# Token-order probabilities, merged operand splits and a 25th block chunk in a hybrid convolution and attention layer

## The chip, the cores and the metric

The kernel runs on one NeuronCore of a Trainium2 chip. The metric is the device time of one execution in microseconds (us). The engines are named as the profile names them: PE multiplies matrices, PEld loads its stationary operand, DVE is the vector engine, ACT the scalar engine, POOL and SP here mostly issue transfers. SBUF is the on-chip memory of 128 partitions, PSUM the eight banks of 128 x 512 float32 into which PE writes.

## The reference

One layer on 512 latent tokens of width 1024 (an 8 x 64 grid) and 256 context tokens. RMS norm and modulation give `h` and `hc`; one input projection gives ten parts; a gated short convolution is branch A, neighbourhood attention branch B; both are projected, merged by sigmoid gates, projected again and added to `x`.

```python
parts = _split_in(h @ w_in)            # b, c, x, z_a, q, k, v, z_b, g_a, g_b: 1024 columns each
q, k = rope(q), rope(k)                # 16 heads of 64
k_c, v_c = split(hc @ w_in[:, K_OFF:V_END])
# query (row r, col c) sees all 8 rows x 16 columns clip(c-8, 0, 48)..+15, and all 256 context keys
p = softmax([q.k_nb * scale + rel_bias, q.k_c * scale])
attn = p_nb @ v_nb + p_c @ v_c
y_a = (silu(z_a) * b * conv3(c * x)) @ w_out_conv
y_b = (silu(z_b) * attn) @ w_out_attn
out = x + gt * rmsnorm((sigmoid(g_a) * y_a + sigmoid(g_b) * y_b) @ w_o)
```

## The kernel before, in words

**Precision.** Every float32 operand is split into a high part H (a rounded copy, type float32r, made on ACT, line 68) and a low part L = x - H (a subtraction on DVE, line 71). A product is then three matmuls, H.H, H.L and L.H. `split` (lines 64 to 76) is that pair of operations, so each split is one ACT and one DVE operation, the second waiting for the first.

**Chunks.** The weights come in chunks of 1024 x 256 (two units of 128 output columns), 40 of them from `win` and 8 from `wout`, in the order that the list `order` writes out. Each chunk is four DMAs on SP's queue into `ring`, which holds one and a half chunks. A plain chunk is split by two 128x1024 operations (`Chunk.split`) and multiplied by `unit`/`proj_T` (lines 174 to 176): per unit 8 x 3 matmuls of 128x512. A block chunk is cut into 2 x 2 blocks (B11, B12, B21, B22), and `pair` forms both units from seven products instead of eight, in the manner of Strassen and Winograd: seven `product` calls of 12 matmuls of 128x256 (line 299). Its operands are B11, B21, the sums T1 and T2 (`Chunk.first`, made ahead of time) and T3, T4, B22 (`Chunk.second`, made when the pair begins); the sums are DVE additions in place in `ring` (lines 112 to 120; line 129 for the chunks below). A pair has a first half (B11, B21, T1, T2, on three banks `a`, `b`, `e`) and a second (T4, T3, B22); ACT copies banks out (lines 310 to 321), DVE adds (lines 316 to 327). Five chunks, of the query and key pairs 1, 2, 3, 4 and 6, also need the plain B12 (`keep`): there B12 must be split before B22 is added to it in place. 24 chunks go in blocks; `paired` decides which.

**Operand buffers.** Split operands lie in four buffers `w` of 128 x 2048: a block chunk takes two in `first` and two in `second`, so those of the next chunk come free as the pair's halves end.

**Attention.** For each pair of heads p (0 to 7) and head h, four blocks b of 128 queries. A query block sees 32 grid columns, which are two key tiles of 128 keys, and two tiles of context keys. The blocks are shifted by 64 queries against the token order, block 3 holding the last 64 and the first 64. `scores` (line 723, 732) multiplies, DVE adds the bias and takes the maximum (line 739), ACT takes the exponential (746, 750) and scales (753). `turn2` transposes the 128x128 pieces on PE (line 760) and splits them into TH and TL, indexed by query block and tile. `gather` multiplies by the values: 12 matmuls (line 779), four of 128x512 for the context and eight of 128x256, each of those over two query blocks that needn't be adjacent; then it adds the two halves of the result on ACT and DVE (784, 785, and 786 for the block that wraps round). `values` splits V in pieces of 128x128, one per head pair and token tile.

**Order.** `plan` lists which projections fill PE between the attention steps of each head pair: the main loop runs one score block, one part of the fill, transposes and gathers in turn. After the loop comes `gate2(3)`, the last gate zb 3, around the last `gather`, then the merge with the gates g 2, g 3, the first output chunk y 0 and so on. Python order is only the starting point: the framework arranges each engine's instructions when the program is built, by its own estimates, and the engines then run these fixed orders, each waiting on semaphores.

Of the kernel before, what the change touches and what calls it, by code (L numbers as in the profile page):

```python
# [27 lines left out]
def layer(ctx: ExitStack, tc, xp, ctxt, ctxT, cc, wmod, small, wfirst, win, wout, wo, rel, tab, out):  # L28
# [59 lines left out]
    class Chunk:  # L88


        def __init__(self, src):
            self.raws = []
            for i in range(2):
                at = 2 * (turn[0] % 3)
                turn[0] += 1
                for o in range(2):
                    nc.sync.dma_start(ring[:, at + o], src[:, 2 * i + o])
                self.raws.append(ring[:, at:at + 2].rearrange("p u (k c) -> p u k c", k=4))
# [8 lines left out]

        def first(self, keep=False):
            (b11, b12), (b21, b22) = self.b = [(r[:, 0], r[:, 1]) for r in self.raws]
            t, sums = (wtile([P, 2, 2, 4, P]) for _ in range(2))  # L110
            split(t[:, 0, 0], t[:, 0, 1], b11)
            nc.vector.tensor_add(b11, b11, b12)
            split(sums[:, 0, 0], sums[:, 0, 1], b11)
            split(t[:, 1, 0], t[:, 1, 1], b21)
            nc.vector.tensor_add(b11, b11, b22)
            split(sums[:, 1, 0], sums[:, 1, 1], b11)
            self.keep = keep
            if not keep:
# [124 lines left out]
    def paired(n, i):  # L243
        return n == "g" or n == "v" and i == 1 or n == "qk" and i in (1, 2, 3, 4, 6) or n == "zb" and i < 3 or n in ("cx", "bz") and i > 3
# [141 lines left out]
    with ExitStack() as p0:  # L386
# [80 lines left out]
        with tc.manual_schedule(engines={E.PE, E.DVE, E.Activation, E.SP}):  # L467
# [58 lines left out]
            kept(1, wide[1])  # L526
# [121 lines left out]
    def values(g):  # L648
        w = chunk()
        for p in (2 * g, 2 * g + 1):  # L650
            V[p] = aw.tile([P, 6, 2, P], F32R, name="V", bufs=3)
        for t in range(6):
            ps = pj()
            n = t % 4
            proj_N(ps, w, hx if t < 4 else hc, slice(n * P, (n + 1) * P))
            vs = summed(ps)
            for i, p in enumerate((2 * g, 2 * g + 1)):
                src = vs[:, i * P:(i + 1) * P].rearrange("p (h d) -> p h d", h=2)
                split(V[p][:, t, :, 0:64], V[p][:, t, :, 64:P], src)
            if t % 2:  # L660
                yield
# [49 lines left out]

    def scores(p, h, b):
# [42 lines left out]

    def turn2(pts, b, TH, TL):
        tps = [psT().rearrange("p (c q) -> p c q", c=4) for _ in pts]
        for tp, pt in zip(tps, pts):
            for c in range(4):
                nc.tensor.transpose(tp[:, c], pt[:, c * P:(c + 1) * P], ident)  # L760
        for n, tp in enumerate(tps):
            split(TH[:, b + n], TL[:, b + n], tp)

    def gather(p, h, TH, TL):
# [12 lines left out]
        for n, (kt, dst, src) in enumerate(work):  # L777
            for t in (TH, TL):
                nc.tensor.matmul(  # L779
                    o3[:, dst], lhsT=V[p][:, kt, h], rhs=src(t),  # L780
                    start=n == 0 and t is TH, stop=n == len(work) - 1 and t is TL,
# [3 lines left out]
        nc.vector.tensor_add(attn[p][r, 64:512], o[r, :448], tmp[r, :448])  # L785
        nc.vector.tensor_add(attn[p][r, 0:64], o[r, 448:], tmp[r, 448:])
# [68 lines left out]
    for i, (p, h, b) in enumerate(blocks):  # L855
# [388 lines left out]
```

## Time and profile before

| | before |
|---|---|
| median of 3 runs | 703.33 us (702.55 to 703.91) |
| the profiled execution, its time and its span | 702.33 us and 700.5 us |
| DVE in 492 to 528 us (zb 3, g 2, g 3) | 31.78 us busy of 36 |
| DVE in 450 to 475 us | 24.75 us busy of 25 |
| granted PE clock, mean | 0.998 |

The profile is of one execution; its span runs from the first to the last instruction, and 1.8 us lie around it. PE's records overlap: a matmul of 128x256 has a record of 283 ns, but in a stream the next one starts about 120 ns later. So start-to-start times are used for PE, and for DVE and ACT either the mean duration of one operation, or the start-to-start time where they follow each other without a wait.

### The profile page before, as it was taken

Reading aid. Unit: us, or ns where it says so; the run is one execution under the profiler, and the core shown is the slowest. Engines: PE = TensorE matmul, PEld = TensorE weight load, DVE = VectorE, ACT = ScalarE, POOL = GpSimd, SP = SyncE. Lnnn points to the kernel's source line nnn. Section 1 sums busy time; section 2 is a strip of 40 time slices with the busy share of each in tenths; the row PEclk is TensorE's granted clock in tenths of the full one; section 3 lists DMA queues with packets and bytes.
Section 4 is the critical chain, followed back from the end, with each engine's and each line's share of the span. In section 5 each row is a group of like instructions: output and inputs, shape, how many; then the busy total and the mean of one; then the engine's idle time right before and its main releaser. Section 6 shows DMA issues by size and latency. Waiting matters only on the chain.

```text
span 700.5 us, 12059 instructions
## 1 busy us (share of the span) xinstructions
PE 690.8 (99%) x4340; PEld 622.7 (89%) x4340; DVE 609.5 (87%) x1184; ACT 448.3 (64%) x905; POOL 66.6 (10%) x110
## 2 busy tenths in 40 slices
PE   7999999999999999999999999999999999999996
PEld 5888888899989999898999989999898899988885
DVE  6999998799898999877999697999799787775996
ACT  7568542677688687675877757787694444442563
POOL 0000003122040310402103113000000000000000
PEclk9999999999999999999999999999999999999999
DMA  9995955347263463543635436334464445660013
GB/s 354 406 350 192 314 168 128 77 114 186 81 152 108 111 181 125 113 144 82 165 119 136 111 104 160 95 112 143 149 222 136 146 146 175 232 235 30 31 61 120
DMA packets 51727, 108.84 MB, mean 155 GB/s; under 512 B 6610, under 2 KB 6866, under 8 KB 51668
## 3 DMA queue, kind: packets, MB, share of 16 engines
q1 hardware_dynamic: 43202, 92.73, 39.1%
q0 software_dynamic: 8320, 15.21, 10.9%
q8 instruction: 34, 0.56, 0.3%
q14 instruction: 25, 0.20, 0.1%
q10 hardware_dynamic: 146, 0.14, 0.1%
HBM read 87.60 MB, written 5.25 MB: 133 GB/s over the span
## 4 chain that ended last, share of the span: by engine, by line
PE 97%; DMA 1%; DVE 1%; SPq 1%; ACT 0%; issue 0%; DVEq 0%; ACTq 0%
PE ps L299 34%; PE ps L174 9%; PE ps L176 9%; PE ps L175 9%; PE ps L187 6%; PE ps L1042 5%; PE ps L779 4%; PE ps L760 4%; PE ps L192 3%; PE ps L723 3%; PE ps L206 2%; PE ps L457 2%; PE ps L463 2%; PE ps L460 2%; DMA wm<-in_wmod 1%; PE ps L732 1%
## 5 line engine op out<-in xcount | busy, mean ns | idle before, releaser
L71 DVE TENSOR_TENSOR w<-ring,w 128x512 fp32r<-128x512 f32 (+1 forms) x215 | 166.0, 789 | 29.8 <-ACT w L68 28.8
L68 ACT CAST w<-ring 128x512 fp32r<-128x512 f32 (+1 forms) x215 | 144.5, 706 | 67.0 <-PE ps L176 21.6
L299 PE MATMUL ps<-S,w 128*128 128x256 f32 x1152 | 146.2, 283 | 0.0
L299 PEld LDWEIGHTS ps<-S,w 128*128 128x128 f32 x1152 | 141.7, 192 | 0.1
L299 PE MATMUL ps<-h,w 128*128 128x256 f32 x864 | 112.5, 284 | 0.0
L299 PEld LDWEIGHTS ps<-h,w 128*128 128x128 f32 x864 | 108.0, 191 | 2.0
L174 PE MATMUL ps<-h,w 128*128 128x512 f32 x144 | 56.4, 391 | 0.0
L175 PE MATMUL ps<-h,w 128*128 128x512 f32 x144 | 56.3, 391 | 0.0
L176 PE MATMUL ps<-h,w 128*128 128x512 f32 x144 | 55.9, 389 | 0.0
L631 POOL DMA_DIRECT2D tc<-tb x32 | 28.6, 1048 | 285.6 <-DVE tc L629 181.7
L753 ACT ACTIVATE pt<-pt,z 128x512 f32<-128x512 f32 x64 | 43.0, 723 | 7.5 <-DVE z L751 7.3
L68 ACT CAST TH<-ps 128x512 fp32r<-128x512 f32 x64 | 35.7, 586 | 13.8 <-PE ps L760 13.7
L71 DVE TENSOR_TENSOR TL<-ps,TH 128x512 fp32r<-128x512 f32 x64 | 42.5, 681 | 0.8 <-ACT TH L68 0.3
L739 DVE CUSTOM_DVE_ANT_1 ps<-ps,bt 128x512 f32<-128x512 f32 x56 | 38.7, 692 | 4.4 <-PE ps L723 4.3
L760 PE MATMUL ps<-ident,pt 128*128 128x128 f32 x256 | 33.3, 273 | 0.0
L187 PE MATMUL ps<-w,h 128*128 128x512 f32 x128 | 32.4, 394 | 0.0
L176 PEld LDWEIGHTS ps<-h,w 128*128 128x128 f32 x144 | 27.0, 188 | 5.7
L175 PEld LDWEIGHTS ps<-h,w 128*128 128x128 f32 x144 | 27.1, 188 | 5.5
L174 PEld LDWEIGHTS ps<-h,w 128*128 128x128 f32 x144 | 27.0, 188 | 5.5
L760 PEld LDWEIGHTS ps<-ident,pt 128*128 128x128 f32 x256 | 29.2, 140 | 2.2 <-ACT pt L753 0.4
L746 ACT ACTIVATE pt<-ps,m 128x512 f32<-128x512 f32 x32 | 22.1, 690 | 13.6 <-DVE m L739 12.9
L779 PE MATMUL ps<-TH,V 128*128 128x256 f32 (+1 forms) x96 | 28.4, 318 | 0.0
(251 smaller groups left out, 1400.5 us busy)
## 6 DMA issues: line engine op xcount, KB each, us to landing
ring<-in_win SPq DMA_DIRECT2D x148, 256.0 KB, 3.2
wm<-in_wmod SPq DMA_DIRECT2D x26, 512.0 KB, 7.4
ring<-in_wout SPq DMA_DIRECT2D x32, 256.0 KB, 3.3
bt<-in_rel SPq DMA_DIRECT2D x16, 256.0 KB, 2.7
tc<-tb POOLq DMA_DIRECT2D x32, 128.0 KB, 3.3
wg<-in_wmod SPq DMA_DIRECT2D x16, 256.0 KB, 3.1
B<-in_wo SPq DMA_DIRECT2D x8, 512.0 KB, 5.9
fraw<-in_wfirst SPq DMA_DIRECT2D x8, 384.0 KB, 8.3
```

The lines of the kernel that those rows point to most:

```text
L68: cast = nc.scalar.copy(H, src)
L71: nc.vector.tensor_sub(L, src, H.bitcast(F32))
L174: nc.tensor.matmul(ps, lhsT=H[k][:, cs], rhs=mH[k], start=k == 0, stop=False)
L175: nc.tensor.matmul(ps, lhsT=H[k][:, cs], rhs=mL[k], start=False, stop=False)
L176: nc.tensor.matmul(ps, lhsT=L[k][:, cs], rhs=mH[k], start=False, stop=k == KT - 1)
L187: nc.tensor.matmul(ps, lhsT=mH[k][:, ts], rhs=both[k].rearrange("p a c -> p (a c)"), start=k == 0, stop=False, skip_group_check=True,)
L299: nc.tensor.matmul(ps, lhsT=w[:, x, k], rhs=act[y][k], start=start and k + o == 0, stop=k == 3 and o == 2, skip_group_check=True,)
L739: nc.vector.tensor_tensor_reduce(out=s3, in0=s3, in1=bt[:, e::4 - e][:, 0:2], scale=-1.0, scalar=3.0e38, op0=ALU.add, op1=ALU.min, accum_o ...
L753: nc.scalar.mul(x, x, z[:, i:i + 1])
L760: nc.tensor.transpose(tp[:, c], pt[:, c * P:(c + 1) * P], ident)
L779: nc.tensor.matmul(o3[:, dst], lhsT=V[p][:, kt, h], rhs=src(t), start=n == 0 and t is TH, stop=n == len(work) - 1 and t is TL,)
L1042: nc.tensor.matmul(out, lhsT=a(x, k, ts), rhs=w[y][k // 2][:, k % 2, cols], start=start and k + o == 0, stop=k == 3 and o == 2, skip_group ...
```

## The change

Four edits, made together:

1. `Chunk.two` splits two operands of a chunk by one operation of 128x1024 instead of two of 128x512: B11 with B21, T3 with T4, and in the five `keep` chunks B12 with B22. It reads both from `ring` with a step, so both have to be there, and what overwrites either has to wait for the whole operation.
2. V: two token tiles are summed side by side and then split by one operation of 128x256 per head pair.
3. `turn2` stores the probabilities in token order (block 3 is transposed against a rotated identity, which POOL makes at the start), `places` lays the key tiles so that every `gather` operand is contiguous, and each inner product covers just the queries that see the tile: 192, 256, 256 and 192 instead of 256 each. The sum at the end is one operation instead of two.
4. `paired` also names zb 3: the last gate chunk goes through `pair` instead of `unit`.

```diff
         def first(self, keep=False):
...
-            split(t[:, 0, 0], t[:, 0, 1], b11)
+            self.B = {"T1": sums[:, 0], "T2": sums[:, 1]}
+            self.two(("B11", "B21"), t, (0, 0))
             nc.vector.tensor_add(b11, b11, b12)
             split(sums[:, 0, 0], sums[:, 0, 1], b11)
-            split(t[:, 1, 0], t[:, 1, 1], b21)
...
+        def two(self, names, x, us):
+            at = [a + u for a, u in zip(self.at, us)]
+            lo = min(at)
+            src = ring[:, lo:max(at) + 1:max(at) - lo].rearrange("p n (k c) -> p n k c", k=4)
+            split(x[:, :, 0], x[:, :, 1], src)
+            for n, a in zip(names, at):
+                self.B[n] = x[:, int(a > lo)]
...
         def second(self):
...
             if self.keep:
-                split(last[:, 1, 0], last[:, 1, 1], b12)
+                self.two(("B12", "B22"), last, (1, 1))
                 nc.vector.tensor_add(b12, b12, b22)
-            for n, x, b in (("T3", t[:, 0], b12), ("T4", t[:, 1], b21), ("B22", last[:, 0], b22)):
-                split(x[:, 0], x[:, 1], b)
-                self.B[n] = x
-            self.B["B12"] = last[:, 1]
+            self.two(("T3", "T4"), t, (1, 0))
+            if not self.keep:
+                split(last[:, 0, 0], last[:, 0, 1], b22)
+                self.B["B22"] = last[:, 0]
...
-        return n == "g" or ... or n == "zb" and i < 3 or n in ("cx", "bz") and i > 3
+        return n == "g" or ... or n == "zb" or n in ("cx", "bz") and i > 3
...
-        work.append((0, slice(0, 4, 3), lambda t: t[:, 0:4:3, 0]))
-        for k in range(1, 3):
-            work.append((k, slice(k - 1, k + 1), lambda t, k=k: t.rearrange("p b c q -> p (b c) q")[:, 4 * k - 3:4 * k + 1:3]))
-        work.append((3, slice(2, 4), lambda t: t[:, 2:4, 1]))
+        for kt, a, b in ((0, 0, 192), (1, 64, 320), (2, 192, 448), (3, 320, S)):
+            work.append((kt, a, b, lambda t, kt=kt, a=a, b=b: t[:, 3 * (kt % 2), a:b]))
...
-        nc.vector.tensor_add(attn[p][r, 64:512], o[r, :448], tmp[r, :448])
-        nc.vector.tensor_add(attn[p][r, 0:64], o[r, 448:], tmp[r, 448:])
+        nc.vector.tensor_add(attn[p][r], o[r], tmp[r])
```

Since the framework arranges the instructions anew, the edits move others too. Three places. In all rows the changed kernel's lines are higher by 2 to 21: 299 becomes 311, 71 becomes 73, 779 becomes 800, 723 becomes 742.

**PE, the gather of head pair 7, head 0.** Before (`TH`, `TL`: the probabilities; `h_82` to `h_85`: tokens for the first product of the next pair, g 1; `S_1242`: the last of the pair ahead, g 0):

```order
L299 MATMUL ps<-S_1242,w 128x256 x3
L779 MATMUL ps<-TH,V 128x512
L723 MATMUL ps<-ks,qd 128x512
L723 MATMUL ps<-ks,qe 128x512
L299 MATMUL ps<-h_82,w 128x256 x3
L299 MATMUL ps<-h_83,w 128x256 x3
L299 MATMUL ps<-h_84,w 128x256 x3
L299 MATMUL ps<-h_85,w 128x256 x2
L779 MATMUL ps<-TL,V 128x512
```

The same place in the changed kernel:

```order
L311 MATMUL ps<-S_1236,w 128x256 x3
L800 MATMUL ps<-TH,V 128x512
L800 MATMUL ps<-TL,V 128x512
L800 MATMUL ps<-TH,V 128x512
L800 MATMUL ps<-TL,V 128x512
L800 MATMUL ps<-TH,V 128x192
L800 MATMUL ps<-TL,V 128x192
```

Two scores and eleven matmuls that stood between the gather's first matmul and its second now stand behind the gather.

**DVE, the split operands for the second half of the chunk of query and key pair 2.** Before (`w_1960` holds B22 and B12, `w_1959` T3 and T4; line 129 is the addition in place to B12, 316 an addition of the running pair):

```order
L71 TENSOR_TENSOR TL_1767<-ps_1946,TH_1766 128x512
L71 TENSOR_TENSOR w_1960<-ring_105,w_1960 128x512
L71 TENSOR_TENSOR w_1959<-ring_105,w_1959 128x512
L129 TENSOR_TENSOR ring_105<-ring_105 128x512
L71 TENSOR_TENSOR w_1960<-ring_105,w_1960 128x512
L316 TENSOR_TENSOR tc_1970<-tc_1970,ps_1973 128x256
L71 TENSOR_TENSOR w_1959<-ring_105,w_1959 128x512
```

Now (`w_1929` holds B12 and B22, `w_1928` T3 and T4):

```order
L73 TENSOR_TENSOR TL_1740<-ps_1915,TH_1739 128x4x2x64
L73 TENSOR_TENSOR w_1929<-ring_106,w_1929 128x2x512
L328 TENSOR_TENSOR tc_1935<-tc_1935,ps_1938 128x256
L140 TENSOR_TENSOR ring_106<-ring_106 128x512
L73 TENSOR_TENSOR w_1928<-ring_106,w_1928 128x2x512
```

T4, which the second half multiplies first, was the second split and stood ahead of the addition; now it is in the last one, behind the addition.

**PE, the second half of g 3, two chunks behind zb 3, and the start of y 0** (`us`: operand of y 0). Before, three whole products, then y 0:

```order
L299 MATMUL ps<-h_86,w 128x256 x3
L299 MATMUL ps<-h_87,w 128x256 x3
L299 MATMUL ps<-h_88,w 128x256 x3
L299 MATMUL ps<-h_89,w 128x256 x3
L299 MATMUL ps<-S_943,w 128x256 x3
```

Now:

```order
L311 MATMUL ps<-h_87,w 128x256 x2
L311 MATMUL ps<-S_947,w 128x256 x2
L311 MATMUL ps<-S_944,w 128x256 x2
L185 MATMUL ps<-us_6073,w 128x512
L311 MATMUL ps<-h_87,w 128x256
L311 MATMUL ps<-h_88,w 128x256 x3
L311 MATMUL ps<-h_89,w 128x256 x3
```

The two matmuls with H of each product stand ahead, with the first of y 0, and the third, which needs L, comes after them. The same break stands in the second halves of query and key pairs 1 and 2. In the kernel before, no product of a pair is broken like this; one (g 1) is parted by a gather.

On SP's queue the loads of g 2 move behind the first half of zb 3, since a pair asks for the next chunk in its middle and a plain chunk at its start. POOL's queue gains one copy at the start and exchanges some neighbours among its transfers.

More of the change, by code (lines that the diff above doesn't have):

```diff
@@ L48, in layer @@
     sp = const.tile([P, 72], F32, name="sp")
-    ident = const.tile([P, P], F32, name="ident")
+    wide = const.tile([P, 192], F32, name="ident")
+    ident, rolled = wide[:, :P], wide[:, 64:]
     make_identity(nc, ident)
+    nc.gpsimd.tensor_copy(wide[:, P:], wide[:, :64])
     eps = const.tile([P, 1], F32, name="eps")
@@ L95, in __init__ @@
                 turn[0] += 1
+                self.at.append(at)
                 for o in range(2):
@@ L213, in proj_c, with summed @@
             )
-    def summed(ps):
-        t = cv.tile([P, S], F32, name="ta")[:, :256]
+    def summed(ps, t=None):
+        if t is None:
+            t = cv.tile([P, S], F32, name="ta")[:, :256]
         nc.scalar.copy(t, ps[:, 256:])
@@ L516, in keep_busy @@
                     nc.tensor.matmul(acc[5][:, :256], lhsT=ident, rhs=cb[:, 0, :256], start=True, stop=True)
-            wide = [spread(i) for i in range(2)]
+            spreads = [spread(i) for i in range(2)]
             square(0)
             square(1)
-            kept(0, wide[0])
+            kept(0, spreads[0])
             root(0)
@@ L525, in layer @@
             norm(1)
-            kept(1, wide[1])
+            kept(1, spreads[1])
             square(2)
@@ L655, in values @@
             proj_N(ps, w, hx if t < 4 else hc, slice(n * P, (n + 1) * P))
[L656 to L659, printed above, removed]
+            if t % 2 == 0:
+                vs = cv.tile([P, 2, 256], F32, name="ta")
+            summed(ps, vs[:, t % 2])
             if t % 2:
+                for i, p in enumerate((2 * g, 2 * g + 1)):
+                    src = vs[:, :, i * P:(i + 1) * P].rearrange("p t (h d) -> p t h d", h=2)
+                    split(V[p][:, t - 1:t + 1, :, 0:64], V[p][:, t - 1:t + 1, :, 64:P], src)
                 yield
@@ L710, in layer @@
     whole = []
+    places = [(0, 3, 1, 2), (3, 0, 1, 2), (0, 3, 1, 2), (0, 3, 1, 2)]
     def scores(p, h, b):
@@ L757, in turn2 @@
         tps = [psT().rearrange("p (c q) -> p c q", c=4) for _ in pts]
-        for tp, pt in zip(tps, pts):
+        for n, (tp, pt) in enumerate(zip(tps, pts)):
             for c in range(4):
-                nc.tensor.transpose(tp[:, c], pt[:, c * P:(c + 1) * P], ident)
+                nc.tensor.transpose(tp[:, places[b + n][c]], pt[:, c * P:(c + 1) * P], rolled if b + n == 3 else ident)
         for n, tp in enumerate(tps):
-            split(TH[:, b + n], TL[:, b + n], tp)
+            if b + n < 3:
+                ts = slice(64 + (b + n) * P, 64 + (b + n + 1) * P)
+                split(TH[:, :, ts], TL[:, :, ts], tp)
+            else:
+                H, L = (t.rearrange("p c (a q) -> p c a q", q=64)[:, :, 0::7] for t in (TH, TL))
+                split(H, L, tp.rearrange("p c (a q) -> p c a q", q=64))
     def gather(p, h, TH, TL):
@@ L769, in gather @@
         o = psO()
-        o3 = o.rearrange("p (b q) -> p b q", b=4)
-        work = [(4, slice(0, 4), lambda t: t[:, :, 2]), (5, slice(0, 4), lambda t: t[:, :, 3])]
-        work.append((0, slice(0, 4, 3), lambda t: t[:, 0:4:3, 0]))
-        for k in range(1, 3):
-            work.append((k, slice(k - 1, k + 1), lambda t, k=k: t.rearrange("p b c q -> p (b c) q")[:, 4 * k - 3:4 * k + 1:3]))
-        work.append((3, slice(2, 4), lambda t: t[:, 2:4, 1]))
-        for n, (kt, dst, src) in enumerate(work):
+        work = [(4, 0, S, lambda t: t[:, 1]), (5, 0, S, lambda t: t[:, 2])]
+        for kt, a, b in ((0, 0, 192), (1, 64, 320), (2, 192, 448), (3, 320, S)):
+            work.append((kt, a, b, lambda t, kt=kt, a=a, b=b: t[:, 3 * (kt % 2), a:b]))
+        for n, (kt, a, b, src) in enumerate(work):
             for t in (TH, TL):
                 nc.tensor.matmul(
-                    o3[:, dst], lhsT=V[p][:, kt, h], rhs=src(t),
-                    start=n == 0 and t is TH, stop=n == len(work) - 1 and t is TL,
+                    o[:, a:b], lhsT=V[p][:, kt, h], rhs=src(t),
+                    start=n == 0 and t is TH, stop=n == len(work) - 1 and t is TL, skip_group_check=True,
                 )
```

9 lines of the change are left out of this document (4 added, 5 removed).

## The prediction

> **What bounds the kernel now.** I read the page's busy times first, then the slices, the chain and PE's waits.
>
> ```profile
> PE 690.8 (99%) x4340; PEld 622.7 (89%) x4340; DVE 609.5 (87%) x1184; ACT 448.3 (64%) x905; POOL 66.6 (10%) x110
> PE   7999999999999999999999999999999999999996
> DVE  6999998799898999877999697999799787775996
> PE 97%; DMA 1%; DVE 1%; SPq 1%; ACT 0%; issue 0%; DVEq 0%; ACTq 0%
> ```
>
> ```profile
> PE ps L507 <- ACT crow L479: 3.7, 1, 3.7
> PE ps L457 <- ACT h L555: 0.3, 1, 0.3
> ```
>
> PE is full from the second slice to the last but one, the chain is PE for 97%, and after the start PE waits for nobody: those two rows are all its waits. So today every nanosecond of matmul counts and no nanosecond of DVE or ACT does. But DVE is at 87%, and at nine tenths or more in 19 of the 40 slices: PE's freedom from waits hangs on DVE finishing in the right order. The change takes from PE, and alters DVE's order and load. Both have to be priced.
>
> What a matmul costs is the distance between starts. From the timeline of PE, in y 3 and the gate chunk g 7 behind it, in a gather, and at transposes:
>
> ```profile
> 599.79 0.39 PE L174 MATMUL ps<-as,w 128*128 128x512 f32 x1
> 601.60 0.39 PE L176 MATMUL ps<-as,w 128*128 128x512 f32 x1
> 601.83 3.04 PE L299 MATMUL ps<-h,w 128*128 128x256 f32 x24
> 604.70 3.04 PE L299 MATMUL ps<-S,w 128*128 128x256 f32 x24
> ```
>
> ```profile
> 184.84 0.40 PE L779 MATMUL ps<-TH,V 128*128 128x512 f32 x1
> 185.77 0.28 PE L779 MATMUL ps<-TH,V 128*128 128x256 f32 x1
> 186.72 0.39 PE L723 MATMUL ps<-ks,qd 128*128 128x512 f32 x1
> ```
>
> ```profile
> 475.04 1.03 PE L760 MATMUL ps<-ident,pt 128*128 128x128 f32 x8
> 475.83 1.68 PE L299 MATMUL ps<-h,w 128*128 128x256 f32 x12
> ```
>
> Between the first two rows lie eight steps: 1.81/8 = 0.226 us for 512 columns. 24 matmuls of 256 take 2.87, so 0.1196 each. In the gather four of 512 take 0.93 (0.2325 each, 0.006 more than elsewhere) and eight of 256 take 0.95 (0.119). Eight transposes of 128 columns take 0.79, 0.099 each.
>
> **PE's share of the change.**
>
> *zb 3 in blocks.* 2 x 24 matmuls of 512 go: 48 x 0.226 = 10.86 us. Seven products of 12 come: 84 x 0.1196 = 10.05. Net -0.81.
>
> *192 columns.* 16 gathers have four of their matmuls narrowed from 256 to 192, 64 in all. No row shows this width in this number format. A straight line through 512 and 256 (0.00042 per column) gives 0.093: -1.7 us in all. If loading the stationary operand sets the pace it stays at 0.119: no gain. The nearest row speaks against the line: transposes have 128 columns, for which the line gives 0.066, but take 0.099. I take the middle between that row and 0.119, which is 0.109: 64 x 0.010 = -0.64. The bad end is the plain float32 rate, which the fillers at the start show:
>
> ```profile
> 11.74 1.03 PE L516 MATMUL ps<-cb,ident 128*128 128x256 f32 x4
> 12.61 0.38 PE L539 MATMUL ps<-ident,x 128*128 128x128 f32 x2
> ```
>
> Four records are two matmuls of 256 columns: 0.87/2 = 0.435 each, or 0.326 for 192; 64 x 0.207 = +13.2 us. That is a rival. The Trainium skill (TensorE: Matmul & The Clock Gate, section Back-to-back issue gap) gives a gap of columns/2.4 + 2.5 ns, 82.5 ns for 192; by that the edit would be worth 64 x 36.5 ns = 2.3 us. The trace disagrees for narrow matmuls: by the rule a transpose would be at 56 ns, its row is at 99.
>
> *Contiguous operands.* 64 matmuls of 512 in the gathers lose at most the 0.006 us: 0 to -0.4, I take -0.2, since the scores, too, read in pieces.
>
> PE alone: -0.81 - 0.64 - 0.2 = -1.65 us. The transposes keep their number and width. POOL's extra copy follows the making of the identity, which PE uses six microseconds later, and costs nothing:
>
> ```profile
> 1.02 0.29 POOL masks.py:199 TENSOR_SCALAR_AFFINE_SELECT ident<-ident 128x128 f32<-128x128 f32 x1
> ...
> 7.40 1.22 PE L516 MATMUL ps<-cb,ident 128*128 128x256 f32 x2
> ```
>
> **DVE's and ACT's share.** Durations by shape, and two runs of splits without waits:
>
> ```profile
> L71 DVE TENSOR_TENSOR w<-ring,w 128x512 fp32r<-128x512 f32 x173 | 114.9, 683 | 10.2 <-ACT w L68 9.5
> L71 DVE TENSOR_TENSOR w<-ring,w 128x1024 fp32r<-128x1024 f32 x42 | 51.1, 1222 | 19.5 <-ACT w L68 19.3
> L68 ACT CAST w<-ring 128x1024 fp32r<-128x1024 f32 x42 | 44.0, 1053 | 24.6 <-PE ps L176 12.4 <-DMA ring<-in_wout 5.4 <-DMA ring<-in_win 4.3
> L71 DVE TENSOR_TENSOR V<-ta,V 128x128 fp32r<-128x128 f32 x48 | 11.9, 285 | 3.3 <-ACT V L68 3.3
> L324 DVE SCALAR_TENSOR_TENSOR tc<-tc 128x256 f32<-128x256 f32 x16 | 6.7, 420 | 3.0 <-ACT tc L321 3.0
> L785 DVE TENSOR_TENSOR at<-ps,ta 64x448 f32<-64x448 f32 x16 | 9.9, 620 | 0.8 <-ACT ta L784 0.6
> ```
>
> ```profile
> 472.39 1.88 DVE L71 TENSOR_TENSOR w<-ring,w 128x512 fp32r<-128x512 f32 x3
> ```
>
> In a stream a DVE operation of 512 holds the engine (1.88 - 0.683)/2 = 0.60 us, its record being 0.08 longer; 1024 hold it 1.222 - 0.08 = 1.14. So a merged split saves 0.06 us of DVE, not half: 24 chunks with two merges and five with a third are 53 x 0.06 = 3.2 us. V saves (0.285 - 0.08) x 48 less 24 x 0.34, the holding time of 256 by the 420 row: 1.7. The gather's second addition goes, about 0.1 each, 1.6 in 16. On PE's path all of this is worth nothing by itself, because PE doesn't wait. What costs is that a merged operand is ready only when both are:
>
> *Query and key pair 2* (second place of the order). Its rows before:
>
> ```profile
> 182.47 0.67 DVE L71 TENSOR_TENSOR TL<-ps,TH 128x512 fp32r<-128x512 f32 x1
> 183.05 1.28 DVE L71 TENSOR_TENSOR w<-ring,w 128x512 fp32r<-128x512 f32 x2
> 187.19 1.58 PE L299 MATMUL ps<-h,w 128*128 128x256 f32 x12
> ```
>
> T4's L was ready at 184.33, 2.9 us before PE wanted it at 187.19. Now there follow on TL: the B12/B22 split 1.14, a running addition 0.34, the addition in place 0.60, then ACT's cast of 1.05 (it may not start before the addition ends) and DVE's split of 1.22. From 183.05 that is 4.35 us plus 0.1 for two handovers: 187.5. One more addition (line 112, now 125) has slipped into the stretch ahead: 188.1; DVE had no gap there before, and each new wait for an ACT cast adds, one or two of up to 1.05: 188.1 to 190. PE has nine matmuls to put ahead, 1.1 us, so it loses 0 to 1.8. I take 1.3, near the upper end, since the wait is in series with a full engine; it also covers the running pair's bank, which comes free later. The other four keep chunks have the same series with more cover: 0 to 0.9 each, I take 0.8 for all. Together 2.1 (0 to 5.4).
>
> *Gather of pair 7, head 0* (first place). Before:
>
> ```profile
> 480.22 0.40 PE L779 MATMUL ps<-TH,V 128*128 128x512 f32 x1
> 481.26 0.67 DVE L71 TENSOR_TENSOR TL<-ps,TH 128x512 fp32r<-128x512 f32 x1
> 482.23 0.40 PE L779 MATMUL ps<-TL,V 128*128 128x512 f32 x1
> ```
>
> TL was ready at 481.93, 1.7 us after the first matmul; two scores and eleven products filled that. Now TL is wanted one matmul after TH, at 480.45. If DVE is as late as before, PE stands 1.5 us; if the shorter queue ahead of TL brings it forward, 0. I take 0.8.
>
> *zb 3, g 2, g 3* (third place). DVE's load from 492 to 528 us, and its waits there:
>
> ```profile
> 492.00:528.00 36.00, 31.78 (x55) 1.00 0.55 190
> ```
>
> ```profile
> DVE us L71 <- ACT us L68: 2.1, 2, 1.7
> DVE g L324 <- ACT g L321: 1.1, 1, 1.1
> ```
>
> zb 3 before: two splits of 1024, 2.28 us. Now: two of 1024 and three of 512 (4.08), four additions in `ring` (2.4), four operations of 256 on the results (1.36): 7.84, so +5.6. Merges in g 2 and g 3 and the gather's addition take back 0.35. 31.78 + 5.2 = 37.0 us of work, while PE's work there shrinks to 35.2. DVE falls behind by 1.8 even without a gap, by 3.4 if half of the 3.2 us of waits above stays; splits for y 0 in the stretch can slip instead. 0 to 3.4, I take 1.9. The loads of g 2, now asked for in the middle of zb 3, add nothing to that:
>
> ```profile
> ring<-in_win SPq DMA_DIRECT2D x148, 256.0 KB, 3.2
> ```
>
> They land 3.2 us after their issue, and the second half of zb 3 (36 x 0.12) and the gather last 6; without that cover g 2's first split would be late by what is lacking.
>
> The Trainium skill (Perfetto Trace Analysis, section Optimizing Scalar/DVE Operations) says both things: grouping into larger operations helps a saturated engine, at about 60 ns of overhead per DVE operation on SBUF; where the engine isn't saturated but makes others wait, breaking up is better. The 0.06 us here agrees with the figure; which half applies is what the places above decide.
>
> **The sum.** Waits 2.1 + 0.8 + 1.9 = 4.8, PE -1.65: +3.15 us. On the profiled execution, 702.33 (700.5 of span and 1.8 around it), that is 705.5. The median of the runs lies 1.0 above it, so 703.33 + 3.15 = 706.5 us.
>
> **The rivals.** About 0.2%, 1.4 us, is what a measurement of this kernel can tell from no change.
>
> *The waits don't come* (faster). DVE loses 6.5 us of work outside zb 3, so it may run ahead and hide the series. For it: no wait of PE in 670 us before, and slices at 7 and 8. Against it: the order puts H matmuls ahead of late L ones in three pairs, where before it did so in none. 703.33 - 1.65 = 701.7, below 701.9. This is the grouping half of that page's rule. It decides if T4 of pair 2 is ready by about 188.4 and DVE catches up by g 3. Chance 0.13.
>
> *Half of it* (the same): waits of 0.3 to 3.0 us, 702 to 704.7. Chance 0.13.
>
> *192 columns at the float32 rate* (much slower): +13.2 instead of -0.64; DVE then has 13 us more room, so most waits go: 703.33 - 1.0 + 13.2 + 1 = 716.5. No row shows a split operand's matmul under 256 columns, so nothing excludes it; that 512 and 256 lie on one line speaks against a jump. Chance 0.07.
>
> *The forecast*, waits of over 3 us: 0.67.
>
> The range: at the low end waits of 0.8 us, 702.5. At the high end, 710.5, they come to 8.8, most of the 10.3 that the upper ends give (5.4 + 1.5 + 3.4). Left out are the best of the fast case and the 192-column rival.
>
> **What would show it.** PE records 4376. In the waits, PE rows that wait for DVE, about 5 us in sum: at the second half of pair 2, at L800 near 480, at L311 and L185 near 525 to 530. DVE busy in the stretch of zb 3 to g 3 near 100%. L800's 192 wide matmuls 0.10 to 0.12 us apart. Wrong would be: no PE waits, a 192 step of 0.09 or of 0.33, or waits at places that I did not name.

## The result and the profile after

| | before | after |
|---|---|---|
| median of the runs | 703.81 us (702.55 to 703.91, 5 runs) | 707.65 us (707.45 to 708.84, 5 runs) |
| the profiled execution, time and span | 702.33 and 700.5 us | 707.47 and 705.7 us |
| ratio | | 1.0062, 95% interval 1.0048 to 1.0076 |

Slower by 0.6%, or 4.4 us (3.4 to 5.4), against a forecast of 3.15. The two profiled executions lie 5.1 apart. The page of the changed kernel: busy times, the slices of PE and DVE, and the chain.

```profile
PE 692.7 (98%) x4376; PEld 623.6 (88%) x4376; DVE 610.9 (87%) x1102; ACT 443.5 (63%) x835; POOL 67.0 (10%) x111
PE   7999999999999999999999999999999999999996
DVE  6999998799797998977998787999999787775996
PE 69%; DVE 20%; ACT 5%; DMA 3%; issue 2%; SPq 0%; DVEq 0%; ACTq 0%
```

PE has its 4376 records and its slices look as before; DVE has 82 operations fewer and is busy 1.4 us longer. The chain tells the difference: it was PE for 97%, and now runs through DVE for a fifth of the span. PE's waits behind the 3.7 us at the start that both kernels have (the kernel before had only one other, of 0.3):

```profile
PE ps L800 <- DVE TL L73: 1.1, 2, 0.8
PE ps L311 <- ACT w L70: 0.8, 2, 0.5
PE ps L469 <- ACT h L567: 0.6, 1, 0.6
PE ps L185 <- ACT w L70: 0.5, 1, 0.5
PE ps L311 <- DVE w L73: 0.3, 1, 0.3
PE ps L779 <- ACT pt L772: 0.2, 1, 0.2
```

(L469 is that one, near the start, now 0.6.) Only 1.4 of these 3.5 us wait for DVE, the rest for ACT. This view shows less than PE loses, because a matmul's record goes on for 0.16 us after the next could start. What follows therefore uses **standing time**: over all matmul records behind the first 100 us, what the distance between two starts exceeds the median for that line and shape, where it exceeds it by over 0.13 us. Before: 0. After: 4.8 us, at twelve places, in us:

| second half of pair 2 (187.3), and transposes behind it (197.6) | 0.70, 0.35 |
|---|---|
| first half of zb 0 (241), second half of pair 4 (274) | 0.25, 0.15 |
| gather at 295 | 0.47 |
| gather of pair 7, head 0 (482.9) | 0.92 |
| g 2, g 3 and the first product of y 0 (516 to 529) | 0.17, 0.41, 0.47, 0.14, 0.61 |
| g 4 (548) | 0.18 |

Each stop costs about another 0.1 us, 1.2 in sum, since the matmul that ends it is followed late (below). The three places of the prediction, in PE's, DVE's and ACT's timelines.

Pair 2:

```profile
184.91 1.22 DVE L73 TENSOR_TENSOR w<-ring,w 128x1024 fp32r<-128x1024 f32 x1
186.04 0.41 DVE L328 TENSOR_TENSOR tc<-tc,ps 128x256 f32<-128x256 f32 x1
186.37 0.69 DVE L140 TENSOR_TENSOR ring<-ring 128x512 f32<-128x512 f32 x1
187.09 1.05 ACT L70 CAST w<-ring 128x1024 fp32r<-128x1024 f32 x1 [1.06 <-DVE ring L140]
188.17 1.23 DVE L73 TENSOR_TENSOR w<-ring,w 128x1024 fp32r<-128x1024 f32 x1 [1.11 <-ACT w L70]
188.19 0.50 PE L311 MATMUL ps<-h,w 128*128 128x256 f32 x2 [0.54 <-ACT w L70]
188.53 0.99 PE L311 MATMUL ps<-S,w 128*128 128x256 f32 x7
189.45 1.45 PE L311 MATMUL ps<-h,w 128*128 128x256 f32 x10
```

That is the series as the prediction lists it: split of B12 with B22, running addition, addition in place, cast of T3 with T4, its subtraction. T4's L part is there at 189.40, forecast for 188.1 to 190. PE stops at 188.19 for the cast, and again at 189.45 for L, by less than the threshold.

The gather of pair 7, head 0:

```profile
482.86 0.39 PE L800 MATMUL ps<-TH,V 128*128 128x512 f32 x1
483.29 0.67 DVE L73 TENSOR_TENSOR TL<-ps,TH 128x512 fp32r<-128x512 f32 x1
484.01 0.50 PE L800 MATMUL ps<-TL,V 128*128 128x512 f32 x1 [0.76 <-DVE TL L73]
484.35 0.39 PE L800 MATMUL ps<-TH,V 128*128 128x512 f32 x1
```

TL is ready at 483.96, 1.1 us after the first matmul, and what filled that time before now stands elsewhere. The third row starts 1.15 us after the first instead of 0.23, and the fourth 0.34 after the third: a stop's tail.

DVE from 492 to 528 us and from 528 to 550 (before: 31.78 and 18.15), and PE at the end of g 3:

```profile
492.00:528.00 36.00, 35.43 (x289) 34.64 (x288) 34.29 (x60) 29.47 (x56) 0.00 (x0) 1.00 0.56 191
528.00:550.00 22.00, 21.53 (x132) 19.05 (x132) 20.07 (x31) 9.07 (x14) 0.00 (x0) 1.00 0.47 157
```

```profile
525.47 0.50 PE L311 MATMUL ps<-S,w 128*128 128x256 f32 x2 [0.26 <-ACT w L70]
526.28 1.47 PE L311 MATMUL ps<-S,w 128*128 128x256 f32 x10 [0.31 <-DVE w L73]
529.15 0.50 PE L185 MATMUL ps<-us,w 128*128 128x512 f32 x1 [0.45 <-ACT w L70]
```

Of the 5.2 us of added work 4.4 show over both stretches, and 2.5 of them in the first, where DVE is at 95%. But these stretches are cut by the clock, and the changed kernel comes to zb 3 over 4 us later. Cut by the work, from the first matmul of zb 3 to the last of g 3, before and after:

```profile
493.90:528.00 34.10, 34.10 (x239) 31.89 (x239) 31.00 (x53) 25.27 (x49) 0.00 (x0) 1.00 0.54 187
498.30:533.10 34.80, 33.78 (x270) 32.57 (x268) 33.73 (x55) 26.79 (x49) 0.00 (x0) 1.00 0.66 224
```

There DVE goes from 91% to 97%.

### The profile page after: what moved, and what is told of

Read it like the earlier page. It is cut to its first block, busy times and chain, and to the rows that moved or that the text cites. A ratio compares the mean times of both kernels' runs of the same rounds, so it can differ in the third digit from the quotient of the medians.

```text
span 705.7 us, 11967 instructions
## 1 busy us (share of the span) xinstructions
PE 692.7 (98%) x4376; PEld 623.6 (88%) x4376; DVE 610.9 (87%) x1102; ACT 443.5 (63%) x835; POOL 67.0 (10%) x111
## 4 chain that ended last, share of the span: by engine, by line
PE 69%; DVE 20%; ACT 5%; DMA 3%; issue 2%; SPq 0%; DVEq 0%; ACTq 0%
PE ps L311 18%; PE ps L185 8%; PE ps L187 8%; PE ps L186 8%; DVE w L73 5%; PE ps L198 5%; PE ps L1062 5%; PE ps L203 3%; PE ps L779 2%; PE ps L800 2%; DVE ps L758 2%; DVE TL L73 2%; ACT w L70 2%; PE ps L742 2%; PE ps L469 2%
## 5 line engine op out<-in xcount | busy, mean ns | idle before, releaser
L70 ACT CAST w<-ring 128x1024 fp32r<-128x1024 f32 (+1 forms) x165 | 142.2, 868 | 97.3 <-PE ps L187 26.8
L73 DVE TENSOR_TENSOR w<-ring,w 128x1024 fp32r<-128x1024 f32 (+1 forms) x165 | 163.1, 993 | 33.9 <-ACT w L70 31.9
L311 PE MATMUL ps<-S,w 128*128 128x256 f32 x1200 | 153.8, 284 | 0.7 <-DVE w L73 0.3
L311 PEld LDWEIGHTS ps<-S,w 128*128 128x128 f32 x1200 | 148.0, 192 | 1.7 <-DVE w L73 0.5
L311 PE MATMUL ps<-h,w 128*128 128x256 f32 x900 | 118.4, 285 | 0.6 <-ACT w L70 0.5
L311 PEld LDWEIGHTS ps<-h,w 128*128 128x128 f32 x900 | 112.7, 191 | 3.4 <-ACT w L70 1.0
L186 PE MATMUL ps<-h,w 128*128 128x512 f32 x128 | 50.1, 391 | 0.0
L185 PE MATMUL ps<-h,w 128*128 128x512 f32 x128 | 50.1, 391 | 0.0
L187 PE MATMUL ps<-h,w 128*128 128x512 f32 x128 | 49.7, 390 | 0.0
L198 PE MATMUL ps<-w,h 128*128 128x512 f32 x128 | 32.5, 395 | 0.0
L187 PEld LDWEIGHTS ps<-h,w 128*128 128x128 f32 x128 | 24.0, 188 | 5.1
L186 PEld LDWEIGHTS ps<-h,w 128*128 128x128 f32 x128 | 24.0, 188 | 5.0
L185 PEld LDWEIGHTS ps<-h,w 128*128 128x128 f32 x128 | 24.0, 188 | 5.0
L800 PE MATMUL ps<-TL,V 128*128 128x512 f32 (+2 forms) x96 | 27.3, 319 | 1.1 <-DVE TL L73 1.1
```

The costliest lines, as they stand in the source:

```text
L70: cast = nc.scalar.copy(H, src)
L73: nc.vector.tensor_sub(L, src, H.bitcast(F32))
L185: nc.tensor.matmul(ps, lhsT=H[k][:, cs], rhs=mH[k], start=k == 0, stop=False)
L186: nc.tensor.matmul(ps, lhsT=H[k][:, cs], rhs=mL[k], start=False, stop=False)
L187: nc.tensor.matmul(ps, lhsT=L[k][:, cs], rhs=mH[k], start=False, stop=k == KT - 1)
L198: nc.tensor.matmul(ps, lhsT=mH[k][:, ts], rhs=both[k].rearrange("p a c -> p (a c)"), start=k == 0, stop=False, skip_group_check=True,)
```

## The experiments

The three named places had come out, and others beside them. Whether the named causes hold is another question. The theories: **A**, the merged operands of edit 1 are late; **B**, zb 3 in blocks overloads DVE; **C**, edit 3 (the gathers in a row) is the loss. Later came **D**: a change of any kind makes the framework lay the engines' orders anew, and the new order has some operand late somewhere; and **G**, about the gathers alone. All runs are compared with the kernel before on the same chip.

**Merged splits alone.** The kernel before with the changed class:

```diff
-            split(t[:, 0, 0], t[:, 0, 1], b11)
+            self.two(("B11", "B21"), t, (0, 0))
...
+            self.two(("T3", "T4"), t, (1, 0))
```

> The kernel before with the merged operand splits alone (edit 1). Theory A, that waits for merged operands are the loss and the order on DVE decides where: slower by 0.5 to 2.5 us, with PE waits in the second halves of query and key pairs. Rival B, that zb 3 in blocks overloads DVE and is the loss by itself: no change, within 0.5 us, no new PE waits. Rival C, that token order is the loss: no change either.

Ratio 1.0022 (1.0013 to 1.0031), +1.5 us. Standing time 2.1, at 189, 198.6, 267 and 517: one of four is the place where A put it. By the view of the waits the other three wait for an operand of a plain chunk, for an addition that frees a bank and for ACT's copy of a bank, none of them for a merged operand.

**zb 3 in blocks alone.**

```diff
-... or n == "zb" and i < 3 or n in ("cx", "bz") and i > 3
+... or n == "zb" or n in ("cx", "bz") and i > 3
```

> The kernel before with zb 3 in blocks alone (edit 4). Theory A: PE gains 0.81 us and loses little, since DVE, 5.6 us more loaded there, still has single operands ready in time: -1 to +0.5 us. Rival B: +1.5 to +3 us, with PE waits near 525 to 530 us as in the changed kernel. Rival C: -0.8 us.

Ratio 1.0005 (0.9996 to 1.0014), +0.4 us, no measurable change. Standing time 1.4 (0.75 and 0.28 of it near 524 and 526) takes back PE's 0.8 and a little more. The longer of the two waits for ACT's copy of a bank (0.59), not for DVE. B is not the loss by itself.

**Token order alone** (edit 3 without 1, 2 and 4).

```diff
-        work.append((0, slice(0, 4, 3), lambda t: t[:, 0:4:3, 0]))
+        for kt, a, b in ((0, 0, 192), (1, 64, 320), (2, 192, 448), (3, 320, S)):
```

> The kernel before with token order and the 192-query products alone (edit 3). Theory A: the gathers' 128 narrow and middle matmuls give 0.7 us, as the rows of the changed kernel show (64 of 0.100 and 64 of 0.125 us against 128 of 0.118); the order changes a little: -1 to +0.5 us. Rival C: +2 us or more. Rival B: -0.7 us.

Ratio 1.0042 (1.0029 to 1.0055), +3.0 us: the dearest of the four, against A, though it takes work from PE and from DVE. Standing time 2.7. The gathers have only 0.7 of it (at 204 and 484); the rest lies at 245, 259, 268 and 473, in halves of pairs that edit 3 doesn't touch. At 245, in the timelines of ACT, DVE and PE:

```profile
243.67 0.58 ACT L75 ACTIVATE qd<-tc 128x448 fp32r<-128x448 f32 x1 [2.23 <-DMA tc<-tb]
244.28 0.62 DVE L76 SCALAR_TENSOR_TENSOR qe<-tc,qd 128x448 fp32r<-128x448 f32 x1 [1.74 <-ACT qd L75]
245.23 0.41 DVE L318 TENSOR_TENSOR tc<-tc,ps 128x256 f32<-128x256 f32 x1
245.70 1.57 PE L301 MATMUL ps<-h,w 128*128 128x256 f32 x11
```

A query's split stands at the head of DVE's queue while a transfer is still under way. DVE idles 1.74 us and the addition that frees PE's bank (L318) stands behind it. DVE isn't short of time here; its order is wrong for this moment. This is where theory D comes from.

**All but the merged splits.** The changed kernel with `Chunk` as before.

```diff
-            self.two(("T3", "T4"), t, (1, 0))
+            for n, x, b in (("T3", t[:, 0], b12), ("T4", t[:, 1], b21), ("B22", last[:, 0], b22)):
+                split(x[:, 0], x[:, 1], b)
```

> The changed kernel with the operand splits made one by one again (edits 2, 3 and 4 stay). Theory A: nearly all waits go, PE's gain of 1.5 us is left: -1.5 to 0 us against the kernel before, and PE waits of under 1 us. Rivals B and C: the loss stays, +2 us or more.

Ratio 1.0028 (1.0019 to 1.0037), +2.0. The merged splits are worth 2.4 of the 4.4, which A would explain; 2.0 stay that it can't. That the 2.4 come by A's cause is not shown by this. Standing time 2.9, 1.0 of it in the gathers at 295 and 483, 1.1 from 525 to 546.

**The series of pair 2 taken apart**, in all five keep chunks:

```diff
             if self.keep:
+                split(t[:, 1, 0], t[:, 1, 1], b21)
                 self.two(("B12", "B22"), last, (1, 1))
                 nc.vector.tensor_add(b12, b12, b22)
-            self.two(("T3", "T4"), t, (1, 0))
+                split(t[:, 0, 0], t[:, 0, 1], b12)
+                self.B["T3"], self.B["T4"] = t[:, 0], t[:, 1]
```

> The changed kernel, but in the chunks that keep T2 for later (the query/key pairs) T4 is split first, before the B12/B22 split, and T3 by itself behind the addition. Theory A (the series split, addition, merged split makes T4 late): the stall at the second half of pair 2 near 188 us goes (1.0 us of start-to-start excess), and the other pairs give some tenths: 4.4 over the kernel before becomes 2.3 to 3.4. Theory D (any edit lays the engines' fixed orders anew, and each laying loses PE at other places where VectorE is full): the stall near 188 goes or shrinks, but others of 0.3 to 1 us come elsewhere, 3 to 5 over the kernel before, and no clear gain over the changed kernel.

Ratio 1.0103 (1.0089 to 1.0117), +7.2: 2.8 worse than the changed kernel. The stop at pair 2 is gone, as both theories had it:

```profile
187.83 0.39 PE L746 MATMUL ps<-ks,qe 128*128 128x512 f32 x1
188.05 1.60 PE L315 MATMUL ps<-h,w 128*128 128x256 f32 x12
```

So the series, whose rows above end in that stop, is its cause in the changed kernel; with the merged splits alone the same series cost only 0.26 there. But standing time rose to 6.2, with 0.5 at 242, 0.6 at 280, 1.3 and 1.2 at the gathers of 296 and 485, and 1.5 from 527 to 531. The gather at 296, PE and DVE:

```profile
295.98 0.67 DVE L132 TENSOR_TENSOR ring<-ring 128x512 f32<-128x512 f32 x1
296.57 1.28 DVE L73 TENSOR_TENSOR TL<-ps,TH 128x512 fp32r<-128x512 f32 x2
297.91 0.50 PE L804 MATMUL ps<-TL,V 128*128 128x512 f32 x1 [0.81 <-DVE TL L73]
```

DVE has a block addition ahead of both TL subtractions, and PE stands until they are done. Neither theory had foreseen a loss of 2.8.

**TL's matmuls last in each gather.** DVE's and ACT's instructions stay in the same order, one for one.

```diff
-        for n, (kt, a, b, src) in enumerate(work):
-            for t in (TH, TL):
+        for t in (TH, TL):
+            for n, (kt, a, b, src) in enumerate(work[i] for i in (0, 2, 1, 5, 3, 4)):
```

> The changed kernel with each gather's six TH matmuls ahead of its six TL matmuls, the wide and the 192-wide alternating; VectorE's and ScalarE's instructions and their order stay exactly as in the changed kernel. Theory G (a gather that wants TL one matmul after TH is the cost at 295 and 483 us): both stalls (0.58 and 1.02 us) shrink by the 0.9 us that five more TH matmuls cover: 0.58 goes and 1.02 falls to about 0.2, so 1.2 to 1.5 less than the changed kernel, 2.9 to 3.2 over the kernel before. Rival (VectorE is late as a whole; the next product that needs it takes the wait over): no more than 0.4 less than the changed kernel. On the width: if the loading of the stationary operand sets a floor of 0.11 us, a 192-wide matmul that follows a 512-wide one still starts its successor after 0.09 us and the narrow ones cost about 0.10 in the mean; without such a floor the 256-wide go back from 0.125 to 0.119.

Ratio 1.0053 (1.004 to 1.0065), 0.6 less than the changed kernel, between G and its rival; the two intervals overlap, so the trace says more here than the time. The stop at 295 is gone, that at 483 is 0.26 instead of 0.92, as G has it: 1.1 us. Standing time fell by only 0.4, since PE then stands at 489, 497 and 515 (0.9 together, where the changed kernel has 0.17). On the width, see the last section.

**The same instructions in another order.** One addition per pair is held at its place in program order:

```diff
-        nc.vector.tensor_add(c1[:, second], c1[:, second], b)
+        tc.keep_in_program_order(nc.vector.tensor_add(c1[:, second], c1[:, second], b))
```

> The changed kernel with the same instructions, one for one; only the additions that take the second half of a running bank to SBUF are held at their place in program order, which moves some 70 of VectorE's 1048 rows. Theories A, B and C (the work and the dependencies that the edits add are the cost): 4.2 to 4.7 over the kernel before, as the changed kernel. Theory D (the order that is laid is the cost): a change of over 1 us with nothing else altered; replaying the order with the durations of the trace gives 2.4 us less than the changed kernel, so about 2 over the kernel before.

(How the 2.4 us there were worked out no run shows.) By name and shape every engine has the same instructions as in the changed kernel; 183 of DVE's 1102 places hold another one than there, 73 of ACT's 835 and 13 of PE's 4376. Ratio 1.0033 (1.002 to 1.0045), +2.3: 2.1 less than the changed kernel, from the order alone, and the intervals don't overlap. D gave 2.4; A, B and C said no change. The gather of pair 7 now has no stop, and a new one stands elsewhere:

```profile
483.37 0.40 PE L802 MATMUL ps<-TH,V 128*128 128x512 f32 x1
483.60 0.39 PE L802 MATMUL ps<-TL,V 128*128 128x512 f32 x1
...
472.84 1.33 PE L313 MATMUL ps<-h,w 128*128 128x256 f32 x9 [0.87 <-DVE tc L341]
```

**DVE's overload moved to GpSimd.** The kernel before with zb 3 in blocks, and in `parts`:

```diff
-            split(t[:, 0], t[:, 1], srcs[k])
+            nc.scalar.copy(t[:, 0], srcs[k])
+            nc.gpsimd.tensor_sub(t[:, 1], srcs[k], t[:, 0].bitcast(F32))
```

> The kernel before with the last zb gate in blocks, and the L subtractions of the splits for y 0 (16 of 128x512, 0.60 us each on VectorE, most of them between 490 and 530 us) on GpSimd. Theory B (VectorE is overloaded there by the 5 us that the gate's blocks add; that overload eats the 0.8 us that PE gains): the stalls near 524 us go and the PE gain shows, 0.5 to 1 less than the kernel before. Rival (GpSimd's subtractions are slow or hold VectorE's port, and y 0 waits for them): the same or up to 2 us more than the kernel before, with PE waits at the first products of y 0.

Ratio 1.0147 (1.0131 to 1.0162), +10.3. Far outside both. GpSimd's and DVE's timelines, PE's, and the granted clock in 40 slices:

```profile
511.00 11.47 POOL L900 TENSOR_TENSOR us<-ur,us 128x512 fp32r<-128x512 f32 x7 [4.35 <-ACT us L899]
```

```profile
510.49 0.69 DVE L792 SCALAR_TENSOR_TENSOR at<-at,tb 128x512 f32<-128x512 f32 x1
511.09 1.79 DVE L791 SCALAR_TENSOR_TENSOR tb<-tb,tc 128x512 f32<-128x512 f32 x1
512.81 1.77 DVE L71 TENSOR_TENSOR w<-ring,w 128x512 fp32r<-128x512 f32 x1
516.64 0.62 PE L299 MATMUL ps<-h,w 128*128 128x256 f32 x3 [3.08 <-DVE g L316]
518.72 3.99 PE L299 MATMUL ps<-S,w 128*128 128x256 f32 x24
PEclk9999999999999999999999999999988999999999
```

While GpSimd subtracts (11.47/7 = 1.64 us each), a DVE operation of 0.69 takes 1.77. DVE has 16 operations fewer than with zb 3 alone and is busy for 620.4 us instead of 615.2. The rival named the mechanism but gave it 2 us. Not all of the 10.3 is waiting: after the stops of 3.2 and 2.7 us the granted clock falls, to 0.64 in the mean from 530 to 534 us, where the other kernels stay at full clock. In two stretches, 517.5 to 520.9 and 531.1 to 537.9, a matmul of 128x256 takes 0.213 us to the next start instead of 0.118, and 24 take 3.99 instead of 3.04 with the clock back at the end. These slow steps are another 3.5 us.

**Merged V splits alone.**

```diff
-                split(V[p][:, t, :, 0:64], V[p][:, t, :, 64:P], src)
+                    split(V[p][:, t - 1:t + 1, :, 0:64], V[p][:, t - 1:t + 1, :, 64:P], src)
```

> The kernel before with the merged V splits alone (1.7 us less of VectorE's work, no operand of a product is wanted sooner). If work were what counts: 0, or a few tenths less than the kernel before. Theory D (every edit lays the fixed order anew, and PE pays where the new order has an operand late): 0.5 to 1.5 over the kernel before, in new stalls at places that this edit doesn't touch. If the costs of the four edits add up, -0.2 to 0.3, since the other three alone gave 0.35, 1.5 and 2.7 and the whole gives 4.4.

Ratio 1.0009 (1.0000 to 1.0018), +0.6: at the lower end of D's range, and the interval begins at no change. Standing time 0.6, at 266 and 516, in pairs of which no instruction was edited. The four edits alone sum to 5.5, each known to 0.6 to 0.9; the whole is 4.4 (3.4 to 5.4). Plain addition is not excluded by the times, but most of the places where PE stands differ from run to run.

**Both alterations that helped**, on the changed kernel: TL last, and the held addition.

```diff
+        tc.keep_in_program_order(nc.vector.tensor_add(c1[:, second], c1[:, second], b))
...
+        for t in (TH, TL):
```

> The changed kernel with both alterations that helped: the gathers' TL matmuls last and wide and narrow alternating (0.85 less than the changed kernel), the additions of the second half held in program order (2.2 less). If the two act at places of their own: 1.2 to 1.6 over the kernel before. If a wait that one removes is taken over by a later one: 2 or more over the kernel before.

Ratio 1.0025 (1.0017 to 1.0034), +1.8, between the two expectations. Standing time 2.9; 0.7 at pair 2, 1.0 at 472 and 0.6 at 525 to 527 stay.

**Splits one by one, and TL last.**

```diff
+            for n, x, b in (("T3", t[:, 0], b12), ("T4", t[:, 1], b21), ("B22", last[:, 0], b22)):
...
+        for t in (TH, TL):
```

> The changed kernel with the splits one by one (2.0 over the kernel before as it stood) and the gathers' TL matmuls last. Two gather stalls of 0.57 and 0.64 us go, and the alternation may give 0.3: 0.8 to 1.2 over the kernel before. If PE's gain from the narrow matmuls and the gate (1.5 us) can come out at all, here it would: 0 to 0.5 less.

Ratio 1.0007 (0.9998 to 1.0017), +0.5, between the two expectations: the gathers' rewrite is worth 1.5 here. Standing time 1.8, of which 1.1 from 524 to 545, eats PE's gain.

**zb 3 in blocks, and the held addition.**

```diff
+... or n == "zb" or n in ("cx", "bz") and i > 3
...
+        tc.keep_in_program_order(nc.vector.tensor_add(c1[:, second], c1[:, second], b))
```

> The kernel before with the last zb gate in blocks (0.35 over the kernel before, 2.0 us of stalls against 0.8 us of PE gained) and the additions of the second half held in program order. Theory D: the change of order alone moves it by some tenths to 1 us either way; the replay of the order gives 0.15 less than without, so 0.2 over. If it beats both kernels it must come 0.7 or more below, with the stall of 0.85 us near 524 gone.

Ratio 1.0009 (0.9999 to 1.0019), +0.6. Standing time 2.5; the stop near 524 grew from 0.75 to 1.0. The addition that helped the changed kernel helps here nothing. No version beat the kernel before.

All runs together. Standing time less PE's gain (0.8 for zb 3, 0.64 for the narrow matmuls) against what the ratio gives, in us:

| kernel | standing | PE gain | difference | measured |
|---|---|---|---|---|
| changed | 4.8 | 1.45 | 3.4 | 4.4 |
| merged splits alone | 2.1 | 0 | 2.1 | 1.5 |
| zb 3 alone | 1.4 | 0.8 | 0.5 | 0.4 |
| token order alone | 2.7 | 0.64 | 2.1 | 3.0 |
| all but merged splits | 2.9 | 1.45 | 1.5 | 2.0 |
| series taken apart | 6.2 | 1.45 | 4.7 | 7.2 |
| TL last | 4.4 | 1.45 | 3.0 | 3.7 |
| held addition | 3.3 | 1.45 | 1.9 | 2.3 |
| zb 3, GpSimd | 8.8 | 0.8 | 8.0 | 10.3 |
| V alone | 0.6 | 0 | 0.6 | 0.6 |
| held and TL last | 2.9 | 1.45 | 1.4 | 1.8 |
| one by one, TL last | 1.8 | 1.45 | 0.3 | 0.5 |
| zb 3, held | 2.5 | 0.8 | 1.7 | 0.6 |

Ten of thirteen measured times lie within 1.0 of the difference. Above it lie the series taken apart, by 2.5, of which the tails of its twelve stops are 1.1, and GpSimd, by 2.3, where the slow clock's 3.5 us aren't counted. The last is 1.1 below. Such misses must be expected: a trace is one execution, and those of one kernel differ by over 1 us (before: 702.55 to 703.91).

## Why the prediction was right, and where it was not

**PE's share, -1.65 forecast.** The width came out at its size: all steps of the gathers, with what exceeds 0.25 us cut off as waits, sum to 29.97 us before and 29.33 after, -0.64, as forecast. But not by the step that was forecast: the 192-wide steps are 0.100 in the mean instead of 0.109, alternately 0.09 and 0.11, and the 256-wide ones between them 0.125 instead of 0.118. That the two make 0.64 is luck. The contiguous operands gave nothing (a 512-wide step 0.231 before, 0.232 after) where -0.2 was taken. For zb 3 alone, measured +0.4 less 1.4 of standing is -1.0 (interval 0.6 each way), against -0.81: it agrees, roughly. So about -1.45.

**The waits, +4.8 forecast.** The measured 4.4 plus 1.45 make 5.8; standing time and tails in the trace are 6.0. By place:

- *Query and key pair 2*: 1.3 forecast. 0.70 at its second half and 0.3 of tails and smaller delays: 1.0. That the series is the cause is shown by its rows and by taking it apart. The other four keep chunks: 0.8 forecast, 0.25 found with its tail, at 274 in pair 4. The stops at 198 (transposes) and 241 (zb 0, which isn't a keep chunk) were not named; they are 0.8 with their tails.
- *Gather of pair 7, head 0*: 0.8 forecast, 1.0 found with its tail. The same at 295, another 0.6, was not named. That it comes from wanting TL one matmul after TH was shown by putting TL last.
- *zb 3 to g 3*: 1.9 forecast, 1.8 of standing and 0.5 of tails. DVE is at 97% of the stretch, near 100% as forecast. But the sum of the work doesn't set the loss by itself: with the addition held DVE has the same work and is as full there, 32.1 of 33.1 us, and PE stands 0.8 instead of 1.8. Which operand comes late decides.

**The step that failed** is the one behind all three: that each wait belongs to its edit, so that an edit's cost can be summed from the places it touches. The V splits and the contiguous gathers were costed at nothing or less; alone they gave +0.6 and +3.0, most of it at places that neither touches. zb 3 was to cost 1.9 - 0.81 = 1.1 and gave 0.4. Taking the series of pair 2 apart was to give back 1.0 to 2.1 by theory A and cost 2.8. And the same instructions in another order gave back 2.1. Two of the prediction's own signs of being wrong came with it: waits at places that it did not name (1.6 us with their tails), and 0.09 us for every other 192-wide step. Of its "about 5 us" of PE rows that wait for DVE, 1.4 came. So the sum is in part luck: what the keep chunks lacked, the unnamed places made up. It came out because every order that was laid anew made PE stand, 0.6 to 8.8 us in all thirteen kernels, where the order before makes it stand 0. Why none came out as well as that is not shown; the kernel before with nothing but its order altered was not run. The forecast that DVE's savings are "worth nothing by itself, because PE doesn't wait" held: no edit that saved DVE work made the kernel faster. One reading was off: DVE is at nine tenths or more in 22 slices of the kernel before, not in 19.

The rival "the waits don't come" rested on that saved work. The trace refutes it by PE's 4.8 us of standing time and by the chain, 20% DVE. The rule of the Trainium skill (Perfetto Trace Analysis, section Optimizing Scalar/DVE Operations) that went with it has two halves, grouping for a saturated engine and breaking up for one that makes others wait. Merged splits alone cost 1.5 us here with DVE at 87%, which agrees with the second half; but only one of their four stops was at a merged operand, so it isn't shown that the size of the operations is what cost.

One cost of merging was named too briefly. DVE's idle time in front of the weight splits, by shape (before: 10.2 in front of 173 of 512, 19.5 in front of 42 of 1024):

```profile
L73 DVE TENSOR_TENSOR w<-ring,w 128x1024 fp32r<-128x1024 f32 x95 | 115.6, 1220 | 31.4 <-ACT w L70 29.8 <-DMA wg<-in_wmod 0.6
L73 DVE TENSOR_TENSOR w<-ring,w 128x512 fp32r<-128x512 f32 x70 | 48.0, 686 | 2.4 <-ACT w L70 2.1
```

33.8 us instead of 29.7: 4.1 us more of waiting, 3.1 of them for ACT's casts, against 3.2 us of work that the merging was to save. With the merged splits alone it is 32.5, nearly all of the added 2.8 for ACT's casts.

## What to carry to other kernels

When one engine never waits and the next is at 87%, the order of the second counts as much as its work: here each edit that made the framework lay it anew cost between 0.4 us (not clear of noise) and 3.0 alone, whatever work it saved. Read a change's worth from the engine that sets the end, then look for the places where its next operand comes late, and measure with the same instructions in another order before the cause is put down to the work. A stop that is mended can come back at another place.

## What the runs showed of the hardware

*A narrow matmul's saving is paid back by its successor.* Loads and matmuls of one gather of the changed kernel (226 to 229 us):

```profile
227.82 0.19 PEld L800 LDWEIGHTS ps<-TH,V 128*128 128x128 f32 x1
228.05 0.19 PEld L800 LDWEIGHTS ps<-TL,V 128*128 128x128 f32 x1
228.16 0.19 PEld L800 LDWEIGHTS ps<-TH,V 128*128 128x128 f32 x1
228.28 0.19 PEld L800 LDWEIGHTS ps<-TL,V 128*128 128x128 f32 x1
```

```profile
228.05 0.25 PE L800 MATMUL ps<-TH,V 128*128 128x192 f32 x1
228.14 0.27 PE L800 MATMUL ps<-TL,V 128*128 128x192 f32 x1
228.25 0.31 PE L800 MATMUL ps<-TH,V 128*128 128x256 f32 x1
228.39 0.28 PE L800 MATMUL ps<-TL,V 128*128 128x256 f32 x1
228.51 0.29 PE L800 MATMUL ps<-TH,V 128*128 128x256 f32 x1
```

The first 192-wide takes 0.09 us to the next start, the second 0.11, and the 256-wide behind it 0.14 where 0.12 is usual. The loads of the narrow ones keep 0.11 to 0.12 apart. With wide and narrow alternating, the 64 narrow steps were 0.088 each but the 512-wide behind one took 0.255 instead of 0.233: the 0.022 come back there too. So a load every 0.11 us looks like the floor: in neither order do two loads of the gathers start less than 0.108 us apart. That it is the load and not something else in step with it was not tried apart, and 18 of the 223 distances between transposes' loads are shorter, down to 0.06. By the formula for one matmul alone in the Trainium skill (TensorE: Matmul & The Clock Gate, section Back-to-back issue gap) 192 columns are 82.5 ns, an estimate, near the 0.088 of a step by itself; the section says itself that the formula leaves out the weight load and is too low for narrow matmuls, and 0.11 is what it costs here.

*A stop has a tail*: the 512-wide matmul that ends a wait of PE has a record of 0.50 us instead of 0.39 to 0.40, and the next starts 0.34 after it instead of 0.23; a 256-wide one has 0.39 instead of 0.28, and 0.22 instead of 0.12. At nearly every stop of all thirteen kernels this is 0.10 to 0.11 us, however long the stop (0.13 to 3.2 us); behind the transposes it is 0.06.

*GpSimd's subtractions slowed DVE*: 1.77 us instead of 0.69 for a DVE operation of 128x512 while GpSimd did subtractions of that size, with all operands in SBUF. Two additions of 128x256 that read PSUM took 0.41 beside them, as elsewhere. GpSimd took 1.28 to 1.34 us for the first of a run and mostly 1.7 for those behind; none ran without DVE beside it, so whether it was slowed as well is not shown.

*The clock fell after long stops*: the two longest stops, 3.2 and 2.7 us, were followed by 3.4 and 6.8 us in which a 256-wide step took 0.213 instead of 0.118. No stop behind the first 100 us in the other twelve kernels is longer than 1.2 us, and no such stretch follows one. That the length decides was not tried.
